# A two-block transformer kernel: latent statistics, state-input steps, one gate tile and two state tables put elsewhere in the second block

## The chip, the cores and the metric

The kernel runs on one core of a Trainium2 chip. The metric is the device time of one execution in microseconds (us). The engines of the core run beside one another and meet only at semaphores: PE (TensorE) multiplies matrices, DVE (VectorE) and ACT (ScalarE) work element by element, POOL (GpSimd) does small and odd work, and SP (SyncE) issues every DMA, in the order of the program. PEld is the loading of weights into PE. The profile also shows the clock that PE was granted: 1.00 is 2.4 GHz, 0.50 is 1.2 GHz.

## The reference

Two blocks follow each other on one sequence of 256 tokens of width 1024. The first (two layers of swiglu, pooling and blockwise attention) is not touched by the change. The second is, cut to what matters here:

```
h = rmsnorm(x) * (1 + scale) + shift
u_s, z_s, q_lat, kv_lat, k_rope, z_m, gl_s, gl_m = split(h @ w_in)
y_s = state_space(u_s)                     # 64 groups, 64 states, chunked scan over time
y_s = ((a * sigmoid(b)) * silu(z_s)) @ w_br_ssm,   [a, b] = gelu(y_s) @ w_glu + b_glu
q = rmsnorm(q_lat) @ w_q_up ;  k, v = rmsnorm(kv_lat) @ w_kv_up      # latent attention
y_m = (attention(q, k, v) * silu(z_m)) @ w_br_mla                    # 16 heads
x = x + gate * rmsnorm((sigmoid(gl_s) * y_s + sigmoid(gl_m) * y_m) @ w_out)
```

All of it is float32. A product of two float32 matrices is made of three matmuls in a reduced format: each operand is split into a high and a low part, and high by high, low by high and high by low are summed in PSUM.

## The kernel before, in words

Activations are held transposed (features on the partitions, 256 tokens along the row). Weights come as tiles of 128x1024 (512 KB): SP loads each into one of five raw buffers (`wraw`, L215), ACT casts the high part (`whi`, L229), DVE subtracts for the low part (`wlo`, L220), and PE uses the pair. `Stream` keeps five raw and five split tiles; a raw buffer is free, and so the next load can be issued, when `wlo` of its tile is done. The order of the tiles is that of the array `w2`, which `prepare` packs. A tile of an ordinary projection (`proj_a`, `mm3`) is 24 matmuls of 256 columns (L356).

`phase2` is the second block. Every engine works through its own list in the order in which the code is written; there is no scheduler. The parts that the change touches, in that order:

1. **The u projection** (L1572 to L1590). Eight weight tiles give `u_s`, in 32 steps p = 0 to 31 of six matmuls each (L368 to L370, `mm3b`), eight steps to each of four column blocks q. Three other things are woven in between these steps. First the statistics of the two latents: `LAT_AT` gives the steps at which the functions of `latent` run. For each latent these are `one` (ACT squares, tiles `stacc` and `stlast`), `two` (`st_half`, PE sums over the partitions, L500), `st_reduce` (PE sums the last square, DVE and POOL make the reciprocal root, L520) and `four` (PE spreads it, L526, DVE and ACT scale the latent and split it into `lhl`). `kfold` (L1539) does the rotary key. Second the state-input steps: `v_steps` is a generator, and `V_RATE[p]` says how many of its steps are taken after step p. For each of four chunks `ch` it has nine steps: four with a group of matmuls of `U` with the table `Gs` (L1554), one with the ACT copy `vt` (L1558), four with a transpose each (L1563); the four ACT copies into `VS` (L1568) and the load of a later table follow with the next step taken. Third `u_evac`: when block q is done, ACT copies it (`us`, L1545) and DVE transposes it into `U` (L1546), which chunk q of the state-input steps reads.
2. **After the last step** the steps that are left run one after the other (L1591 to L1593): all of chunk 3.
3. **The attention** (`mla`). Keys and values are projected from `lhl` (L356 to `mKT`, L368 to `mV`). Then the loop over four groups of heads mixes projections of queries (`q_half`), of the gate z_m (`zm`, eight tiles with psC, L356, then ACT L1873 and DVE L1875) and of the other gate (`gm`) with the steps of sixteen heads (`adv`: scores and softmax, transposition, product with the values L1840). The recurrence of the states runs on POOL beside it (L1600 to L1604).
4. **The branch projection and the z_s projection** (`br_evac`, `zs_step`). `y_mm(ch)` (L1644, L1649) multiplies `U` with the triangular tables `TT[ch // 2]` and the states with the tables `Hs`; it is called in `br_evac` for ch 0 to 2 and in `zs_step` for ch 3 to 7. `TT[0]` and `TT[1]` (`Ta`) are loaded during the attention, `TT[2]` and `TT[3]` (`Tb`) in this part; each takes eight loads (`tload`, L1803) after a memset by POOL (L1618). `tload` of `Tb` is called one at a time in `br_evac` for `TT[2]` and two at a time in `zs_step` for `TT[3]`, so it stands in SP's list among the weight loads and the loads of `Hs` (L1622).

Of the kernel before, what the change touches and what calls it, by code (L numbers as in the profile page):

```python
# [8 lines left out]
F32 = mybir.dt.float32  # L9
# [4 lines left out]
OP = mybir.AluOpType  # L14
# [10 lines left out]
LAG = 1  # L25
LEAD = 7
GRAW = 7
V_RATE = [0] * 9 + ([2, 1] * 3 + [0] * 2) * 2 + [2, 1] * 3 + [0]
HQ = (1, 4)
LAT_AT = (0, 5, 6, 7, 9, 10, 14, 16, 19)  # L30
W_OUT = (1.2, 1.6, 1.5, 1.6)
KV_A = 97
AT_A, AT_Q, AT_O = 150, 0, 2
# [53 lines left out]
def prepare(I):  # L87
# [48 lines left out]
    zmh, quh, gmh = _pack_a(zm), _pack_a(qu), _pack_a(gm)  # L136
    mix = [quh[:1]]
    for i in range(4):
        mix += [zmh[2 * i:2 * i + 1], quh[i + 1:i + 2], zmh[2 * i + 1:2 * i + 2], gmh[i:8 if i == 3 else i + 1]]
    gl = I["w_glu_2"][0].reshape(2, 8, 4, 16, 2048).transpose(0, 2, 1, 3, 4).reshape(1024, 2048)  # L140
    glt = _tiles_a(np.ascontiguousarray(gl))
    glt = glt.reshape(2, 8, 8, 128, 128).transpose(1, 0, 2, 3, 4)
    A["w2"] = np.concatenate(
        [_pack(np.ascontiguousarray(_tiles_a(np.concatenate([ql, kl, krd], 1)).transpose(1, 0, 2, 3))
               .reshape(-1, 128, 128)), _pack_b(us, 256), _pack_a(kn), _pack_b(vv, 512)]
        + mix + [_pack_a(I["w_br_mla_2"][0]), _pack_a(zs), _pack_a(gs),
                 _pack(np.ascontiguousarray(glt).reshape(-1, 128, 128)),
                 _pack_a(I["w_br_ssm_2"][0]), _pack_b(I["w_out_2"][0], 512)], 0)
# [102 lines left out]
class Kernel:  # L251
# [1206 lines left out]
    def phase2(self):  # L1458
# [116 lines left out]
        for q in range(4):  # L1575
            pa = [self.ps("A"), self.ps("B")]
            for k in range(8):
                if k % 4 == 0:
                    hi, lo = self.next()
                p = 8 * q + k  # L1580
                if p in hooks:
                    hooks[p]()
                for x in range(2):
                    self.mm3b(pa[x][:, :256], hp[0][:, k, x], hp[1][:, k, x],
                              flat(hi[:, 2 * (k % 4):2 * (k % 4) + 2]),
                              flat(lo[:, 2 * (k % 4):2 * (k % 4) + 2]), k == 0, k == 7)
                for _ in range(V_RATE[p]):
                    next(vs, 0)
            self.defer(u_evac, q, pa)
        self.flush()  # L1590
        for _ in vs:  # L1591
            pass
        p2v.close()  # L1593
# [1 line left out]
        with self.tc.tile_pool(name="mla", bufs=1) as self.ap:  # L1595
            m = [self.ap.tile([128, 2, 32], F32, name="rm%d" % i, bufs=2) for i in range(2)]
            ar = self.A8[:, 0:1].to_broadcast([128, 2, 32])
            for c in range(31):
                x = XS[:, c]
                PL.tensor_mul(m[0], x, ar)  # L1600
                PL.tensor_mul(m[1][:, 0], x[:, 1], self.A8[:, 1])
                PL.tensor_mul(m[1][:, 1], x[:, 0], self.A8[:, 2])
                PL.tensor_add(m[0], m[0], VS[:, c])
                PL.tensor_add(XS[:, c + 1], m[0], m[1])  # L1604
            PL.tensor_copy(VS[64:, :, 0], XS[:64, :, 1])
            PL.tensor_copy(XS[:64, :, 1], XS[64:, :, 0])
            PL.tensor_copy(XS[64:, :, 0], VS[64:, :, 0])
            self.mla(hh, ll, krs, MM, yy)
        p2a.close()
        pb_ = self.pool("p2b")  # L1610
        zz = pb_.tile([128, KB, T], F32, name="zzs")
# [2 lines left out]
        with self.tc.tile_pool(name="ssy", bufs=2) as sy:  # L1614
            HH = {}
            for c2 in (2, 3):
                TT[c2] = sy.tile([128, 4, 4, 128], F32, name="Tb%d" % c2, bufs=1)
                nc.gpsimd.memset(TT[c2].rearrange("p b j x -> p (b j x)"), 0.0)  # L1618

            def hload(ch):  # L1620
                HH[ch] = sy.tile([128, 2, 512], F32, name="Hs", bufs=3)
                nc.sync.dma_start(HH[ch].rearrange("p b x -> p (b x)"),  # L1622
                                  self.Hd[ch].rearrange("a n g x -> (a n) (g x)"))
            for ch in range(3):
                hload(ch)

            def zs_evac(n, p):
                t = self.tmp.tile([128, T], F32, name="sg", bufs=2)
                S.activation(t, p, AF.Tanh, scale=0.5)
                self.los()  # L1630
                V.scalar_tensor_tensor(zz[:, n], t, 1.0, p, op0=OP.add, op1=OP.mult)
            YF = sy.tile([128, KB, T], F32, name="YF", bufs=1)
            Y = {}

            def y_mm(ch):
                ih, c4 = divmod(ch, 4)
                if c4 == 0:
                    Y[ih] = sy.tile([128, 8, 8, 16], F32, name="YS", bufs=1)
                py = self.ps("A")
                p4 = py[:, :256].rearrange("p (b x) -> p b x", b=2)  # L1640
                for bx in range(2):
                    b = 2 * ch + bx
                    for j in range(4):
                        nc.tensor.matmul(p4[32 * j:32 * j + 32, bx], U[:, 4 * b + j], TT[ch // 2][:, ch % 2 * 2 + bx, j],  # L1644
                                         start=True, stop=False)
                    for j in range(4):
                        q, g2 = divmod(j, 2)
                        x = (g2 * 2 + q) * 128
                        nc.tensor.matmul(p4[32 * j:32 * j + 32, bx], XS[:, :, g2, 2 * b + q],  # L1649
                                         HH[ch][:, bx, x:x + 128], start=False, stop=True)  # L1650
                S.copy(Y[ih][:, :, 2 * c4:2 * c4 + 2].rearrange("p t b x -> p b t x"),
                       p4.rearrange("p b (t x) -> p b t x", t=8))
                if ch + 3 < 8:
                    hload(ch + 3)

            def y_tr(ih):
                for t4 in range(2):
                    pt = self.ps("B")
                    for t in range(4):
                        nc.tensor.transpose(pt[:, t * 128:(t + 1) * 128],  # L1660
                                            Y[ih][:, 4 * t4 + t].rearrange("p b x -> p (b x)"), self.ident)
                    dst = YF[:, 4 * ih:4 * ih + 4].rearrange("p j (c t) -> p t j c", t=8)
                    S.copy(dst[:, 4 * t4:4 * t4 + 4], pt.rearrange("p (t j c) -> p t j c", t=4, j=4))

            GA = {}

            def gelu(i):
                if i:
                    b = sy.tile([128, T], F32, name="gb")
                    S.activation(b, GA[i - 1], AF.Tanh, scale=0.7978845608028654)  # L1670
                if i < KB:
                    a = GA[i] = sy.tile([128, T], F32, name="ga")
                    S.activation(a, YF[:, i], AF.Square)
                self.los()
                if i:
                    g = GA.pop(i - 1)
                    V.scalar_tensor_tensor(g, b, 1.0, YF[:, i - 1], op0=OP.add, op1=OP.mult)
                if i < KB:
                    V.tensor_scalar(a, a, 0.044715, 1.0, op0=OP.mult, op1=OP.add)
                    V.tensor_mul(a, a, YF[:, i])  # L1680
                if i:
                    self.hilo(gg[:, i - 1], g, 0.5)

            def br_evac(n, p):
                V.scalar_tensor_tensor(MM[:, n], MM[:, n], 1.0, p, op0=OP.add, op1=OP.mult)
                self.tload(2, n)
                if n in (3, 5, 7):
                    y_mm(n // 2 - 1)
            self.proj_a(yy, br_evac, tags="CD", late=True)
            self.dump("d_MM", MM)  # L1690

            def zs_step(n, p):
                if n < 4:
                    self.tload(3, 2 * n)
                    self.tload(3, 2 * n + 1)
                if n < 5:
                    y_mm(n + 3)
                if n in (2, 6):
                    y_tr(n // 4)
                zs_evac(n, p)  # L1700
                if n >= 4:
                    gelu(n - 4)
            self.proj_a(hh, zs_step, tags="CD", late=True)

            def gs_evac(n, p):
                S.activation(tg[:, n], p, AF.Tanh, scale=0.5)
                if n < 5:
                    gelu(n + 4)
            self.proj_a(hh, gs_evac, tags="CD", late=True)
# [92 lines left out]
        src = self.Rd[0:16, 4 * c2:4 * c2 + 4, :, :128 - 16 * s]  # L1802
        self.nc.sync.dma_start(tt[16 * s:16 * s + 16, :, 16 * s:], src.rearrange("p b j x -> p (b j) x"))  # L1803

    def mla(self, hh, ll, krs, MM, yy):
        nc, V, S = self.nc, self.nc.vector, self.nc.scalar
        ap = self.ap
        KT = ap.tile([128, 16, T], F32, name="mKT")
# [11 lines left out]
                S.copy(VM[:, th, nch * 512:(nch + 1) * 512], pp[th])  # L1820
        self.proj_b(ll[:, 2:], 2, v_evac, kb=2)
        scale = 96.0 ** -0.5
        Q, Z, P, PT, PO = {}, {}, {}, {}, {}

        def s1(hd):
            sm = self.softmax_a(self.ps("A"), Q[hd], KT[:, hd], 1, lambda th: scale, None)
# [41 lines left out]
            return p[:, :T]  # L1868

        def zm(n):  # L1870
            p = tile8()
            t = self.tmp.tile([128, T], F32, name="sg", bufs=2)
            S.activation(t, p, AF.Tanh, scale=0.5)  # L1873
            Z[n] = ap.tile([128, T], F32, name="zm", bufs=3)
            V.scalar_tensor_tensor(Z[n], t, 1.0, p, op0=OP.add, op1=OP.mult)  # L1875

        def gm(n):
            p = tile8()
# [19 lines left out]
        q_half(0, 0)  # L1898
        q_half(0, 1)
        for grp in range(4):  # L1900
            zm(2 * grp)
            adv()
            if grp < 3:
                q_half(grp + 1, 0)
# [44 lines left out]
```

## Time and profile before

| | |
|---|---|
| median of three runs | 1303.39 us (1303.3 to 1306.41) |
| profiled execution, its own time | 1308.08 us |
| its span, first to last instruction | 1306.3 us |
| PE / PEld busy | 1258.7 us (96%) / 1167.4 us (89%) |
| DVE / ACT / POOL busy | 1015.6 (78%) / 669.4 (51%) / 165.3 us (13%) |
| mean clock granted to PE | 0.987 |
| DMA | 331.14 MB, mean 253 GB/s |

PE's busy time counts overlapping matmuls and is not PE at its peak. What a stage can give is read from PE's waits and from the clock in that stage. A row of the timeline gives start, duration, engine, line and what is worked on, and behind it, in brackets, the time that the engine stood still just before and what ended it. The second block's part that is touched lies between 950 and 1200 us of the span.

### The profile page before, as it was taken

What the parts mean: (1) busy time and instruction counts of PE and PEld (TensorE: products, weight loads), DVE (VectorE), ACT (ScalarE), POOL (GpSimd) and SP (SyncE); (2) the same over time, 40 slices, a digit from 0 to 9 for tenths busy, and PEclk for the clock granted to TensorE, in tenths of its full rate; (3) what the DMA queues carried; (4) which work ended last, traced back from release to release, by engine and by line L of the source; (5) the groups of instructions that cost most, each with busy time, mean ns of one, the idle gap of its engine ahead of it and who ended that gap; (6) DMA issues with size and microseconds to landing.
All of it is one profiled execution on the core that took longest, in us unless ns stands there. A gap on an engine that the chain in (4) does not pass through costs nothing.

```text
span 1306.3 us, 25415 instructions
## 1 busy us (share of the span) xinstructions
PE 1258.7 (96%) x9870; PEld 1167.4 (89%) x9870; DVE 1015.6 (78%) x1768; ACT 669.4 (51%) x1170; POOL 165.3 (13%) x285
## 2 busy tenths in 40 slices
PE   7999999999999999999998999999999899989998
PEld 5999988899988779999886899998888888989997
DVE  6789896789999789999977777878853576537774
ACT  4455444555444665544447555444465855437443
POOL 1000011100002000121111201000210791100000
PEclk9999999899999999999999999999998999989999
DMA  9899996788899568998974478778655544764852
GB/s 365 297 344 386 335 369 237 251 310 259 274 326 332 203 256 299 312 324 301 360 279 145 129 237 268 265 258 282 223 195 172 156 130 124 226 202 143 292 191 81
DMA packets 119850, 331.14 MB, mean 253 GB/s; under 512 B 28273, under 2 KB 39409, under 8 KB 119666
## 3 DMA queue, kind: packets, MB, share of 16 engines
q1 hardware_dynamic: 119730, 329.52, 73.4%
q8 instruction: 77, 1.26, 0.4%
q14 instruction: 43, 0.35, 0.1%
HBM read 317.94 MB, written 10.49 MB: 251 GB/s over the span
## 4 chain that ended last, share of the span: by engine, by line
PE 71%; DVE 4%; ACT 4%; issue 2%; DMA 2%; POOL 1%; SPq 0%; DVEq 0%; ACTq 0%; POOLq 0%
PE psD L356 13%; PE psB L356 12%; PE psA L356 11%; PE psC L356 7%; PE psA L363 5%; PE psB L363 4%; PE psA L364 3%; PE psB L364 2%; DVE wlo L220 1%; PE psA L368 1%; PE psA L369 1%; PE psA L370 1%; PE psB L368 1%; PE psB L370 1%; PE psB L369 1%
## 5 line engine op out<-in xcount | busy, mean ns | idle before, releaser
L220 DVE TENSOR_TENSOR wlo<-wraw,whi 128x1024 fp32r<-128x1024 f32 x391 | 481.3, 1236 | 44.6 <-ACT whi L229 43.4
L229 ACT CAST whi<-wraw 128x1024 fp32r<-128x1024 f32 x391 | 403.1, 1049 | 94.5 <-ACT whi L229 32.7
L356 PE MATMUL psA<-hhl,whi 128*128 128x256 f32 x960 | 247.4, 283 | 4.7 <-ACT hhl L534 4.6
L356 PE MATMUL psB<-hhl,whi 128*128 128x256 f32 x976 | 248.4, 281 | 0.0
L356 PE MATMUL psD<-hhl,whi 128*128 128x256 f32 x1120 | 213.7, 283 | 0.4 <-ACT hhl L534 0.4
L356 PEld LDWEIGHTS psA<-hhl,whi 128*128 128x128 f32 x960 | 180.2, 189 | 7.9 <-ACT hhl L534 6.2
L356 PEld LDWEIGHTS psB<-hhl,whi 128*128 128x128 f32 x976 | 183.8, 190 | 0.0
L389 DVE SCALAR_TENSOR_TENSOR junk<-graw,cb 128x1024 bf16<-128x1024 f32 x146 | 179.3, 1228 | 5.5 <-DMA cb<-in_c 5.5
L356 PEld LDWEIGHTS psD<-hhl,whi 128*128 128x128 f32 x1120 | 178.6, 190 | 2.7 <-issue 1.8
L356 PE MATMUL psD<-hhl,wlo 128*128 128x256 f32 x560 | 157.2, 281 | 0.0
L356 PE MATMUL psB<-hhl,wlo 128*128 128x256 f32 x488 | 136.9, 281 | 0.0
L356 PE MATMUL psA<-hhl,wlo 128*128 128x256 f32 x480 | 134.9, 281 | 1.3 <-DVE wlo L220 1.3
L363 PE MATMUL psA<-shl,whi 128*128 128x512 f32 x352 | 123.8, 392 | 0.0
L356 PEld LDWEIGHTS psD<-hhl,wlo 128*128 128x128 f32 x560 | 106.3, 190 | 0.0
L364 PE MATMUL psA<-shl,wlo 128*128 128x256 f32 x352 | 99.2, 282 | 0.0
L356 PE MATMUL psC<-hhl,whi 128*128 128x256 f32 x480 | 93.4, 286 | 0.4 <-DVE hhl L1456 0.4
L356 PEld LDWEIGHTS psA<-hhl,wlo 128*128 128x128 f32 x480 | 91.2, 190 | 1.7 <-DVE wlo L220 1.7
L356 PEld LDWEIGHTS psB<-hhl,wlo 128*128 128x128 f32 x488 | 92.4, 189 | 0.0
L363 PE MATMUL psB<-shl,whi 128*128 128x512 f32 x264 | 92.2, 390 | 0.0
L484 POOL TENSOR_TENSOR stacc<-stacc,stsq 128x256 f32<-128x256 f32 x33 | 35.1, 1063 | 381.9 <-ACT stsq L479 340.4
L356 PEld LDWEIGHTS psC<-hhl,whi 128*128 128x128 f32 x480 | 77.0, 191 | 3.2 <-issue 2.2
L363 PEld LDWEIGHTS psA<-shl,whi 128*128 128x128 f32 x352 | 66.1, 188 | 14.3 <-issue 0.8
(453 smaller groups left out, 2362.1 us busy)
## 6 DMA issues: line engine op xcount, KB each, us to landing
wraw<-in_win SPq DMA_DIRECT2D x176, 512.0 KB
graw<-in_ada SPq DMA_DIRECT2D x173, 512.0 KB
wraw<-in_w SPq DMA_DIRECT2D x93, 512.0 KB
wraw<-in_wout SPq DMA_DIRECT2D x88, 512.0 KB
wraw<-in_wkv SPq DMA_DIRECT2D x16, 512.0 KB
hg<-in_ada SPq DMA_DIRECT2D x11, 512.0 KB
Hd<-ct SPq DMA_DIRECT2D x64, 64.0 KB
Gd<-gsb SPq DMA_DIRECT2D x16, 256.0 KB
```

Source lines behind the costliest of these rows:

```text
L220: self.nc.vector.tensor_sub(lo, raw, hi.bitcast(F32))
L229: self.nc.scalar.copy(hi, raw)
L356: self.nc.tensor.matmul(*a, skip_group_check=shared, **kw)
L363: mm(out, hi[:, b], a.rearrange("p x t -> p (x t)"), start=first, stop=False)
L364: mm(out[:, :T], lo[:, b], a[:, 0], start=False, stop=last)
L368: mm(out, ah, whi, start=first, stop=False)
L369: mm(out, ah, wlo, start=False, stop=False)
L370: mm(out, al, whi, start=False, stop=last)
L389: self.nc.vector.scalar_tensor_tensor(junk, self.gemv_tile(j), 1.0, self.cb, op0=OP.mult, op1=OP.mult, accum_out=self.modc[:, j:j + 1])
L484: (eng or nc.gpsimd).tensor_add(acc, acc, sq)
```

## The change

The steps of the latent statistics that come after the squares are put later (`LAT_AT`). The state-input steps begin two steps later and come two at a time where they came as 2, 1, 2, 1 (`V_RATE`). The first tile of the gate z_m is computed right after the u projection, into psC, with the rest of the state-input steps inside it, and no longer at the beginning of the attention loop; its evacuation is a function of its own, `zm_evac`, its three buffers lie in the pool `p2a`, and its weight tile stands in `w2` right behind those of u. The last block of u is evacuated directly, not by `defer`. `br_evac` asks for two parts of a `Tb` table in each of its eight calls, `TT[2]` in the first four and `TT[3]` in the last four; `zs_step` asks for none.

```diff
-V_RATE = [0] * 9 + ([2, 1] * 3 + [0] * 2) * 2 + [2, 1] * 3 + [0]
+V_RATE = [0] * 11 + [2, 2, 1, 0, 0, 2, 2, 0] * 2 + [2, 2, 1, 0, 2]
-LAT_AT = (0, 5, 6, 7, 9, 10, 14, 16, 19)
+LAT_AT = (0, 9, 10, 11, 13, 14, 19, 21, 24)
...
-        mix += [zmh[2 * i:2 * i + 1], quh[i + 1:i + 2], zmh[2 * i + 1:2 * i + 2], gmh[i:8 if i == 3 else i + 1]]
+        mix += [zmh[2 * i:2 * i + 1] if i else zmh[:0], quh[i + 1:i + 2], zmh[2 * i + 1:2 * i + 2],
+                gmh[i:8 if i == 3 else i + 1]]
...
-               .reshape(-1, 128, 128)), _pack_b(us, 256), _pack_a(kn), _pack_b(vv, 512)]
+               .reshape(-1, 128, 128)), _pack_b(us, 256), zmh[:1], _pack_a(kn), _pack_b(vv, 512)]
...
-            self.defer(u_evac, q, pa)
-        self.flush()
+            if q < 3:
+                self.defer(u_evac, q, pa)
+        z0 = self.ps("C")
+        hi, lo = self.next()
+        u_evac(3, pa)
+        for k in range(KB):
+            for _ in range({0: 2, 5: 5}.get(k, 0)):
+                next(vs, 0)
+            self.mm3(z0[:, :T], hi, lo, k, hh[:, k], k == 0, k == 7)
+        Z = {}
+        self.zm_evac(Z, pa_, 0, z0[:, :T])
         for _ in vs:
             pass
...
             def br_evac(n, p):
                 V.scalar_tensor_tensor(MM[:, n], MM[:, n], 1.0, p, op0=OP.add, op1=OP.mult)
-                self.tload(2, n)
+                for x in range(2):
+                    self.tload(2 + n // 4, n % 4 * 2 + x)
...
             def zs_step(n, p):
-                if n < 4:
-                    self.tload(3, 2 * n)
-                    self.tload(3, 2 * n + 1)
                 if n < 5:
                     y_mm(n + 3)
...
+    def zm_evac(self, Z, pool, n, p):
+        t = self.tmp.tile([128, T], F32, name="sg", bufs=2)
+        self.nc.scalar.activation(t, p, AF.Tanh, scale=0.5)
+        Z[n] = pool.tile([128, T], F32, name="zm", bufs=3)
+        self.nc.vector.scalar_tensor_tensor(Z[n], t, 1.0, p, op0=OP.add, op1=OP.mult)
...
         for grp in range(4):
-            zm(2 * grp)
+            if grp:
+                zm(2 * grp)
             adv()
```

How the instructions stand on PE behind the last step of the u projection, before. The first row is that step's last matmul, `Gs,U` is chunk 3's group of state-input matmuls (the profile counts each of them as two), `k_ident,vt` its transposes, `lhl,whi` the beginning of the key projection:

```order
L370 MATMUL psB<-whi,hp_11835 128x256
L1554 MATMUL psD<-Gs,U 32x128 x16
L1563 MATMUL psD<-k_ident,vt 128x128 x4
L356 MATMUL psC<-lhl,whi 128x256
L356 MATMUL psC<-lhl,wlo 128x256
```

The same place on PE now; `psC<-hhl` is the gate tile, and lines are one to fifteen higher:

```order
L371 MATMUL psB<-whi,hp_11835 128x256
L1564 MATMUL psD<-k_ident,vt 128x128 x4
L357 MATMUL psC<-hhl,whi 128x256
L357 MATMUL psC<-hhl,wlo 128x256
...
L357 MATMUL psC<-hhl,whi 128x256
L1555 MATMUL psD<-Gs,U 32x128 x16
L357 MATMUL psC<-hhl,whi 128x256
...
L1564 MATMUL psD<-k_ident,vt 128x128 x4
L357 MATMUL psC<-lhl,whi 128x256
```

Five eighths of the gate tile stand between the last step of u and chunk 3's group, and three eighths between this group and its transposes. The first four transposes are chunk 2's; two of them stood among the steps of u before.

How SP's list stands from the end of the branch projection on, before. `Tb_13849` is `TT[3]`, its first load is 16x2048 and its last 16x16x16:

```order
L1622 DMA Hs<-Hd 128x1024
L215 DMA wraw<-in_w 128x1024
L1803 DMA Tb_13849<-Rd 16x2048
L1803 DMA Tb_13849<-Rd 16x16x112
L1622 DMA Hs<-Hd 128x1024
L215 DMA wraw<-in_w 128x1024
L1803 DMA Tb_13849<-Rd 16x16x96
L1803 DMA Tb_13849<-Rd 16x16x80
L1622 DMA Hs<-Hd 128x1024
L215 DMA wraw<-in_w 128x1024
L1803 DMA Tb_13849<-Rd 16x16x64
```

The same loads on SP now; the first `Hs` row here is two `Hs` loads earlier in the list than the first row above:

```order
L1632 DMA Hs<-Hd 128x1024
L216 DMA wraw<-in_w 128x1024
L1811 DMA Tb_13849<-Rd 16x2048
L1811 DMA Tb_13849<-Rd 16x16x112
L216 DMA wraw<-in_w 128x1024
L1811 DMA Tb_13849<-Rd 16x16x96
L1811 DMA Tb_13849<-Rd 16x16x80
L1632 DMA Hs<-Hd 128x1024
L216 DMA wraw<-in_w 128x1024
L1811 DMA Tb_13849<-Rd 16x16x64
L1811 DMA Tb_13849<-Rd 16x16x48
```

All eight loads of `TT[3]` moved ahead of the last three loads of `Hs`, by four weight loads.

## Rows read from the trace of the kernel before

**Rows 1.** Waits of PE, 950 to 1200 us: total us, times, longest us.

```profile
PE psD L1563 <- ACT vt L1558: 2.6, 2, 1.5
PE psD L1840 <- ACT smpt L909: 2.2, 2, 1.3
```

**Rows 2.** Busy time by stretch: us, PE, PEld, DVE, ACT, POOL, clock, DMA share, GB/s.

```profile
974.00:978.00 4.00, 1.90 (x10) 1.50 (x9) 1.22 (x1) 3.90 (x9) 0.00 (x0) 0.84 0.25 102
978.00:982.00 4.00, 4.00 (x16) 3.13 (x16) 0.00 (x0) 1.41 (x2) 0.00 (x0) 0.50 0.43 131
982.00:986.00 4.00, 4.00 (x19) 4.00 (x20) 2.17 (x4) 0.74 (x2) 2.29 (x2) 0.50 0.24 51
986.00:990.00 4.00, 4.00 (x50) 3.02 (x48) 2.62 (x5) 1.44 (x4) 0.00 (x0) 0.88 0.52 174
```

**Rows 3.** Timeline of PE, u projection: start, duration, line, work, wait before it.

```profile
976.74 1.01 PE L500 MATMUL psC<-ones,stacc 128*128 128x1 f32 x4 [2.09 <-ACT stacc L473]
...
995.11 0.28 PE L368 MATMUL psA<-whi,hp 128*128 128x256 f32 x1
...
995.92 0.64 PE L1554 MATMUL psD<-Gs,U 128*32 128x128 f32 x16
996.49 0.39 PE L368 MATMUL psA<-whi,hp 128*128 128x256 f32 x1
...
997.39 0.43 PE L1554 MATMUL psD<-Gs,U 128*32 128x128 f32 x8
997.75 0.43 PE L526 MATMUL psC<-k_ident,strs 128*128 128x128 f32 x2
```

**Rows 4.** Timeline of ACT in the u projection and behind it.

```profile
976.56 0.43 ACT L471 ACTIVATE stlast<-lat 128x256 f32<-128x256 f32 x1
...
1012.82 2.46 ACT L1568 COPY VS<-psD 64x256 f32<-64x256 f32 x4
```

**Rows 5.** Timeline of PE behind the last step of u.

```profile
1012.24 0.28 PE L370 MATMUL psB<-whi,hp 128*128 128x256 f32 x1
1013.77 1.08 PE L1554 MATMUL psD<-Gs,U 128*32 128x128 f32 x32 [1.26 <-issue]
1015.94 0.66 PE L1563 MATMUL psD<-k_ident,vt 128*128 128x128 f32 x4 [1.09 <-ACT vt L1558]
1016.36 0.37 PE L356 MATMUL psC<-lhl,whi 128*128 128x256 f32 x1
```

**Rows 6.** Chain that ended last, start of the attention loop: start, duration, what.

```profile
1032.68 2.81 PE psC L356 x24
...
1036.35 0.28 DVE smx L884
```

**Rows 7.** Timeline of DVE, same place.

```profile
1032.67 1.35 DVE L1894 TENSOR_TENSOR mQ<-psD,CS 64x512 f32<-64x512 f32 x2 [1.11 <-ACT mQ L1893]
```

**Rows 8.** Timeline of PE, z_s projection, groups of y_mm.

```profile
1151.51 0.43 PE L1644 MATMUL psA<-Ta,U 128*32 128x128 f32 x8
...
1155.55 0.43 PE L1644 MATMUL psA<-Tb,U 128*32 128x128 f32 x8
...
1169.04 0.65 PE L1644 MATMUL psA<-Tb,U 128*32 128x128 f32 x8 [4.55 <-DMA Tb<-Rd]
...
1175.60 0.43 PE L1644 MATMUL psA<-Tb,U 128*32 128x128 f32 x8
```

**Rows 9.** Timeline of SP, z_s projection.

```profile
1157.55 0.91 SPq L1803 DMA_DIRECT2D Tb<-Rd  x2
...
1165.05 0.92 SPq L1803 DMA_DIRECT2D Tb<-Rd  x2
```

**Rows 10.** Busy time by stretch, branch and z_s projections.

```profile
1126.00:1138.00 12.00, 12.00 (x127) 11.71 (x126) 5.82 (x8) 4.01 (x5) 0.79 (x1) 1.00 1.00 269
1150.00:1162.00 12.00, 12.00 (x171) 11.13 (x169) 2.87 (x3) 1.82 (x4) 0.00 (x0) 1.00 1.02 294
```

**Rows 11.** Timeline of POOL, memsets of the Tb tables.

```profile
1123.22 3.57 POOL L1618 MEMSET Tb<- 128x2048 f32 x2 [39.82 <-DVE sf L1844]
```

More of the change, by code (lines that the diff above doesn't have):

```diff
@@ L1607, in phase2 @@
             PL.tensor_copy(XS[64:, :, 0], VS[64:, :, 0])
-            self.mla(hh, ll, krs, MM, yy)
+            self.mla(hh, ll, krs, MM, yy, Z, pa_)
         p2a.close()
@@ L1803, in tload, with mla @@
         self.nc.sync.dma_start(tt[16 * s:16 * s + 16, :, 16 * s:], src.rearrange("p b j x -> p (b j) x"))
-    def mla(self, hh, ll, krs, MM, yy):
+    def zm_evac(self, Z, pool, n, p):
[3 more added lines that the diff above has]
+        self.nc.vector.scalar_tensor_tensor(Z[n], t, 1.0, p, op0=OP.add, op1=OP.mult)
+    def mla(self, hh, ll, krs, MM, yy, Z, zpool):
         nc, V, S = self.nc, self.nc.vector, self.nc.scalar
@@ L1822, in mla @@
         scale = 96.0 ** -0.5
-        Q, Z, P, PT, PO = {}, {}, {}, {}, {}
+        Q, P, PT, PO = {}, {}, {}, {}
         def s1(hd):
@@ L1870, in zm @@
         def zm(n):
[L1871 to L1875, printed above, removed]
+            self.zm_evac(Z, zpool, n, tile8())
         def gm(n):
```

## The prediction

> **What bounds the kernel now.** I read PE's waits in the stretch of the change first, then the clock stretch by stretch, then the timeline of PE at each wait, and only then the engines that PE waits for. In most of the stretch PE runs without a gap at 2.4 GHz; what the change can give back is where it does not, and there are four such places.
>
> First, the u projection. Behind step 4 PE stands still for 2.09 us until ACT has the first square of a latent [rows 3], and right behind this gap the granted clock falls to 0.50 and stays low for some ten us [rows 2]. Second, two waits for the ACT copy `vt`, 2.6 us in all, the longer (1.5) inside the u projection and the other 1.09 behind it [rows 1, 5]. Third, chunk 3 of the state input runs alone behind the last step of u: from 1012.4 (1012.24 and one matmul pitch) to 1016.36 PE works 1.1 + 0.4 us and stands still for 1.26 + 1.09 [rows 5]. Fourth, one group of `y_mm` waits 4.55 us for the last two loads of `TT[3]` [rows 8], which SP issued only at 1165.05, 7.5 us after the pair before [rows 9]; in between stands a weight load in SP's list, so the tables are late by the order, not by the transfer.
>
> **Part 1, the statistics.** The sum that stopped PE moves from step 5 to step 9. A step is six matmuls; with the seam to a group it takes 0.81 us (995.11 to 995.92 [rows 3]), without it about 0.71, so from 974.65, where PE stopped (976.74 less 2.09), four steps end at 977.5. ACT was done with the first square when it began the second at 976.56 [rows 4]. The wait goes, with 0.9 us to spare: -2.1. What is next late is POOL's root, which PE needs two steps later, as before, now with two groups of state input in between; I price it at nothing, and at most at one wait like the one removed (+2).
>
> With the wait goes what followed it. Time lost to the clock is the stretch times one minus the clock: 4 x (0.16 + 0.50 + 0.50 + 0.12) = 5.1 us [rows 2]. This stretch held almost only matmuls back to back, so lost clock was lost time: -5.1. The whole part: -7.2. Bounds: -2.1 if the clock falls anyway, -7.5 if some pieces beside it shrink too.
>
> The trace shows the clock falling behind a gap of 2.09 us, while the gap of 1.5 us and the pair of 1.26 and 1.09 left it at 1.00. The Trainium skill (TensorE: Matmul & The Clock Gate, Why this matters for your kernels) blames only gaps longer than this one for throughput drops within a kernel. By that rule the slow stretch would have another cause and the part would give 2.1, not 7.2. The rows decide for 7.2 in the sum; the other result is the first rival.
>
> **Part 2, steps in bunches.** A group of 16 matmuls between two steps: from step to step 995.11 to 996.49, 1.38 us. A group of 8: 996.49 to 997.75, 1.26 us [rows 3]. Without the 0.71 of the step (0.81 less the seam of 0.1) that is 0.67 and 0.55. A chunk had 16 + 8 + 8 = 1.77 and has 16 + 16 = 1.34, three chunks: -1.3. The transposes come as 2, 2 and not as 1, 2, 1; they cost 0.1 to 0.2 each way and I leave them at nothing. Bounds 0 and -1.8.
>
> **Part 3, the waits for `vt` inside u.** Before: 1.5 us, in chunk 1. Now two steps without state input lie between the copy and the transposes, 1.4 us for a copy of 0.6. But ACT takes its list in order: in chunk 0 the copies of the scaled latent stand ahead of `vt`, in chunk 2 the four `VS` copies (2.46 us together [rows 4]) and a cast do. Laying the rows' durations one behind the other I get a wait of 0.6 in the first and 0.4 in the last. 1.5 goes, 1.0 comes: -0.5. Bounds -1.5 and +1.5 (two waits as long as the longest of before).
>
> **Part 4, the gate tile.** A tile is 2.81 us [rows 6]. Behind the last step of u PE now has a pair of transposes (0.2), the tile, chunk 3's group (1.1 and 0.2 for seams), four transposes (0.4), and the wait for `vt`. ACT's chain there is two `us` copies, the four `VS` copies of 2.46 and `vt` of 0.6, begun some 0.9 us later behind a cast: it ends about when the tile does, so 0.2 of wait is left. Sum 4.9 against 4.0 before: +0.9 until the key projection begins. In return the attention loop begins without 2.81 of PE. It does not give all: the first softmax needs the queries, and DVE ends their second product at 1034.02 (1032.67 + 1.35 [rows 7]), while the first maximum began at 1036.35, behind the gate tile's evacuation [rows 6]. ACT and DVE carry the chain from there to the product with the values, where PE waits 1.3 [rows 1]; so the gain is 1036.35 - 1034.05 = 2.3. Net -1.4. Bounds: +0.9 (the loop gains nothing) and -2.35 (all that PE stood still in [rows 5]).
>
> **Part 5, the tables.** All loads of `TT[3]` are issued by the end of the branch projection, and POOL's memsets end at 1126.8 [rows 11], long before the first of them. The wait of 4.55 goes. So does what the clock lost: from group to group 1169.04 to 1175.60 = 6.56 us, where the same work took 1151.51 to 1155.55 = 4.04 [rows 8]: 2.5. Together -7.1. Nothing is late in its place by my reading: the last two `Hs` loads stay where they were relative to PE, with fewer loads ahead of them. The cost is on the DMA engines, busy at 1.00 while the branch projection runs [rows 10]: eight loads of 16 to 128 KB, 576 KB in all, are 2.0 us at the 294 GB/s of [rows 10], in a stage whose weights are asked for up to ten tiles ahead (five raw, five split). Taken as nothing. Bounds of the part 0 and -7.1.
>
> **Sum.** -7.2 - 1.3 - 0.5 - 1.4 - 7.1 = -17.5 us. The profiled execution took 1308.08 (its span 1306.3 and 1.8 around it), 4.7 above the median; the change would make it 1290.6. The terms are differences within one execution, so I take them off the median: 1303.39 - 17.5 = **1285.9 us**.
>
> **Rivals.** *The clock is not given back in u*: the short waits of part 3 and the thin sums bring it down again at another place, or its cause was not the gap. For it: PE's gaps there were many; against: gaps of 1.5 and of 1.26 and 1.09 did nothing. 1285.9 + 5.1 = 1291.0. *The attention loop takes the tile back*: with no gate tile as cover, PE waits for the queries and then for the values; the 2.3 are lost, 1288.2, and 1291 if the wait for the values (1.3) grows to the two us behind which the clock fell. For it: ACT and DVE carry that chain; against: they lose the tile's evacuation and a split as well. *The table wait changes its name*: `y_mm` waits for `Hs` or for ACT's evacuation for half as long: 1285.9 + 3.5 = 1289.4. Against: these loads are issued early and the queue is emptier. *Slower, the weights starve*: the eight loads moved into the branch projection hold the DMA queue there, and the weight loads behind them come late. A load costs at most 3.1 us, from the end of SP's last pair at 1165.97 to PE's restart at 1169.04 [rows 8, 9]. Were each to push the full queue back by that, 24.8 us: 1285.9 + 24.8 = 1310.7. It decides from 17.5 / 8 = 2.2 us a load on. Against: 0.25 us each by bytes, and the lead. The rows of these loads have 512 bytes or less (64 to 448 for all but the first). The Trainium skill (DMA: Bandwidth & Descriptors, Specifications) says that transfers below 512 B miss line rate; no row here gives their share of the engines, and only this raises the rival from next to nothing.
>
> **How the numbers follow.** My forecast, 1285.9 give or take 3: 0.55. Everything at its better bound, some 3.5 further down, 1282: 0.08. Clock in u: 0.13. Attention loop: 0.12. Table wait renamed: 0.08. Starved weights: 0.03; the last 0.01 for no effect. Half-clock stretches outside the change can move a few us from run to run, so the range goes from 1280 to 1293. Faster, that is by over 0.3% (3.9 us, about what a measurement of this kernel tells from no change): 0.95; within it 0.02; slower 0.03.
>
> **What would show it.** In the trace after: no gap before L501 in the u projection and a clock of 1.00 from its first step to its last; groups of 16 there, each under 0.7 us; waits for `vt` under a microsecond; the key projection beginning some 8 to 9 us earlier than 1016.4, and the wait for the values still about 1.3; no wait for `Tb` and 4.0 us from group to group of `y_mm`. I am wrong if the clock is below 1 anywhere in u, if a wait for `Hs`, `wraw` or `wlo` shows up from the branch projection on, or if the attention loop gives back less than a microsecond.

## The result, and the profile of the changed kernel

The changed kernel takes 1289.28 us (median of four executions, 1285.92 to 1290.54), the kernel before on the same chip 1303.35 (four, 1301.05 to 1306.41): a ratio of 0.9889, 95% interval 0.9866 to 0.9911, or 14.1 us less (11.6 to 17.5 by that interval). Forecast were 1285.9, that is 17.5 less, and a range of 1280 to 1293. The profiled execution of the changed kernel took 1289.56 us, its span is 1287.7, its mean granted clock 0.994. PE is busy for 1250.8 us (97%), PEld 1161.1, DVE 1014.7, ACT 669.0, POOL 168.5.

The waits of PE of half a us or more that are left between 950 and 1200 us are these (what waits and for whom: us in total, times, longest us):

```profile
PE psD L1854 <- ACT smpt L910: 1.3, 1, 1.3
PE psC L357 <- ACT mKT L1829: 0.9, 1, 0.9
PE psA L880 <- DVE mQ L1904: 0.7, 1, 0.7
PE psD L1564 <- ACT vt L1559: 0.6, 1, 0.6
PE psD L357 <- ACT VS L1569: 0.5, 1, 0.5
```

The 2.09 for `stacc` [rows 3] and the 4.55 for `Tb` [rows 8] are gone, and of the two waits for `vt` [rows 1] one of 0.6 is left. The stretch that ran at half clock [rows 2] reads now (us, PE, PEld, DVE, ACT, POOL, clock, DMA share, GB/s):

```profile
974.00:978.00 4.00, 4.00 (x33) 3.66 (x31) 2.32 (x2) 4.00 (x9) 0.00 (x0) 1.00 0.05 6
978.00:982.00 4.00, 4.00 (x51) 3.41 (x54) 2.15 (x4) 1.78 (x4) 2.28 (x2) 1.00 0.77 261
982.00:986.00 4.00, 3.51 (x38) 3.11 (x30) 2.77 (x5) 1.30 (x4) 0.00 (x1) 1.00 0.48 145
```

PE in the u projection, behind it and in the z_s projection (start, duration, line, work, and in brackets the wait before it), against [rows 3, 5, 8]:

```profile
954.45 0.38 PE L357 MATMUL psD<-hhl,whi 128*128 128x256 f32 x1 [0.35 <-ACT hhl L535]
...
976.25 0.50 PE L501 MATMUL psC<-ones,stacc 128*128 128x1 f32 x4
...
986.16 0.44 PE L1564 MATMUL psD<-k_ident,vt 128*128 128x128 f32 x2 [0.64 <-ACT vt L1559]
...
989.32 0.64 PE L1555 MATMUL psD<-Gs,U 128*32 128x128 f32 x16
...
1002.16 0.66 PE L1564 MATMUL psD<-k_ident,vt 128*128 128x128 f32 x4
1002.57 0.36 PE L357 MATMUL psC<-hhl,whi 128*128 128x256 f32 x1
...
1004.56 1.08 PE L1555 MATMUL psD<-Gs,U 128*32 128x128 f32 x32
...
1006.75 0.60 PE L1564 MATMUL psD<-k_ident,vt 128*128 128x128 f32 x4
1007.10 0.36 PE L357 MATMUL psC<-lhl,whi 128*128 128x256 f32 x1
...
1024.22 0.49 PE L880 MATMUL psA<-mKT,mQ 128*128 128x128 f32 x2 [0.75 <-DVE mQ L1904]
...
1038.26 0.65 PE L1854 MATMUL psD<-smpt,mV 128*64 128x256 f32 x2 [1.29 <-ACT smpt L910]
...
1140.10 0.42 PE L1654 MATMUL psA<-Ta,U 128*32 128x128 f32 x8
...
1144.14 0.43 PE L1654 MATMUL psA<-Tb,U 128*32 128x128 f32 x8
...
1153.02 0.43 PE L1654 MATMUL psA<-Tb,U 128*32 128x128 f32 x8
...
1157.03 0.43 PE L1654 MATMUL psA<-Tb,U 128*32 128x128 f32 x8
```

The sums of the squares run without a wait (976.25). The gate tile fills what stood empty between the last step of u and the key projection, which now begins at 1007.10. On DVE the first maximum of the attention loop begins 11.0 us earlier than in [rows 6]:

```profile
1025.35 0.29 DVE L885 TENSOR_REDUCE smx<-psA 128x1 f32<-128x128 f32 x1 [0.53 <-PE psA L883]
```

SP issues the last two loads of `TT[3]` 28.3 us earlier than in [rows 9]:

```profile
1136.71 1.19 SPq L1811 DMA_DIRECT2D Tb<-Rd  x2
```

Walking from mark to mark gives the balance of the two profiled executions. The first mark, a matmul ahead of the change, stood at 955.53 in the trace of before:

```profile
955.53 0.39 PE L356 MATMUL psD<-hhl,whi 128*128 128x256 f32 x1 [0.36 <-ACT hhl L534]
```

So 1.1 us was there already at 954.45. The key projection is 9.3 earlier (1016.36 [rows 5]), the first maximum 11.0, the first group of `y_mm` shown 11.4, the last 18.6 (1175.60 [rows 8]). Part by part: u and what lies behind it -8.2, the start of the loop -1.7, the rest of the attention -0.4, the tables -7.2, and the 1.1 that is not the change's. The spans differ by 18.6, the touched stretch by 17.5.

### The profile page after: what moved, and what is told of

It is laid out like the page before. It is cut to its first block, busy times and chain, and to the rows that moved or that the text cites. A ratio compares the mean times of both kernels' runs of the same rounds, so it can differ in the third digit from the quotient of the medians.

```text
span 1287.7 us, 25411 instructions
## 1 busy us (share of the span) xinstructions
PE 1250.8 (97%) x9870; PEld 1161.1 (90%) x9870; DVE 1014.7 (79%) x1768; ACT 669.0 (52%) x1170; POOL 168.5 (13%) x285
## 3 DMA queue, kind: packets, MB, share of 16 engines
q8 instruction: 77, 1.26, 0.4%
## 4 chain that ended last, share of the span: by engine, by line
PE 70%; ACT 4%; DVE 4%; issue 2%; DMA 2%; POOL 1%; SPq 0%; DVEq 0%; ACTq 0%; POOLq 0%
PE psD L357 13%; PE psB L357 12%; PE psA L357 11%; PE psC L357 7%; PE psA L364 5%; PE psB L364 4%; PE psA L365 3%; PE psB L365 2%; DVE wlo L221 1%; PE psA L369 1%; PE psA L370 1%; PE psA L371 1%; PE psB L371 1%; PE psB L370 1%; PE psB L369 1%
## 5 line engine op out<-in xcount | busy, mean ns | idle before, releaser
L596 ACT CAST shl<-sf 128x256 fp32r<-128x256 f32 x88 | 35.8, 407 | 85.9 <-DVE sf L594 85.9
```

Of the source, the lines that this page charges most:

```text
L596: nc.scalar.copy(ss[:, i, 0], s)
```

## The experiments

Twelve runs follow, two of them of the kernels before and after as they are, each timed beside the kernel before on the same chip. Ratios are to that, with their 95% interval; 0.001 is 1.3 us, and gains in us are worked out from the ratios. Where two ratios are compared, the difference is uncertain by some 0.003, or 4 us. In eight of the others a single part was put into the kernel before, or taken out of the changed one; the two named last go beyond the change.

**The kernel before, once more.** No edit.

> The kernel before, unchanged, to see how much of its time differs from run to run. Theory (the clock differs from run to run): ratio within 0.997 to 1.003 of itself, single executions 1301 to 1308 us, and an execution is longer by what its granted clock is lower: 1.3 us for each 0.001 of the mean clock. In the trace the two gaps (2.1 us before L500 in the u projection, 4.5 us before L1644) are there again, and the half-clock stretches behind them may be shorter than the 10 and 7 us of the first profile, or absent. Rival (the profile of before was typical, and the 4 us between its own time and the median come from elsewhere): the same half-clock stretches, 10 and 7 us, in this trace too, and a mean clock of 0.987 in every execution.

1303.82 us, ratio 0.9995 [0.9982, 1.0009]. Its profiled execution took 1303.14 us at a clock of 0.993. The gap is the same, and behind it the clock (first a row of PE's timeline, then stretches as above):

```profile
974.67 0.61 PE L500 MATMUL psC<-ones,stacc 128*128 128x1 f32 x4 [2.09 <-ACT stacc L473]
```

```profile
974.00:978.00 4.00, 3.33 (x20) 2.87 (x20) 1.22 (x1) 3.08 (x6) 0.00 (x0) 0.87 0.31 89
978.00:982.00 4.00, 4.00 (x29) 3.87 (x31) 2.68 (x5) 1.13 (x4) 2.29 (x2) 0.70 0.29 93
1010.00:1014.00 4.00, 3.17 (x16) 3.17 (x17) 0.00 (x0) 2.94 (x6) 0.74 (x3) 0.64 0.18 39
1014.00:1018.00 4.00, 3.75 (x29) 3.53 (x29) 1.24 (x1) 3.83 (x10) 3.33 (x9) 0.94 0.85 163
```

Behind the 2.09 the clock took 4 x (0.13 + 0.30) = 1.7 us and not 5.1; and behind the pair of 1.25 and 1.1, which did nothing in the first trace, it took another 1.7. What a gap costs in clock differs from one execution to the next. Over the 61 executions of before that belong to these runs the median is 1304.81 us at a clock of 0.989 (1297.72 to 1309.81); the 9 at 0.987 took 1307.15 on the mean, the 4 at 0.993 took 1301.16. That is 1.0 us for each 0.001 of clock, where 1.3 was expected, and a wider spread than expected.

**The statistics alone.**

```diff
-LAT_AT = (0, 5, 6, 7, 9, 10, 14, 16, 19)
+LAT_AT = (0, 9, 10, 11, 13, 14, 19, 21, 24)
```

> Only the statistics are moved (LAT_AT of the changed kernel, all else as before). Theory (gap brings the clock down): no gap before L500, clock 1.00 through the u projection, 7.2 us less than an execution like the profiled one; against the median of before 3 to 7 us less (ratio 0.9945 to 0.998). Rival (the slow clock has another cause): the gap goes but the clock falls in the u projection all the same, 2.1 us less (0.998 to 0.999).

1306.04 us, ratio 1.0011 [0.9997, 1.0025]: nothing gained. The 2.09 goes, but PE waits elsewhere:

```profile
977.56 0.65 PE L1554 MATMUL psD<-Gs,U 128*32 128x128 f32 x16 [1.58 <-DVE U L1546]
...
988.83 0.65 PE L1554 MATMUL psD<-Gs,U 128*32 128x128 f32 x16 [1.87 <-issue]
```

```profile
988.02 0.71 DVE L1546 STREAM_TRANSPOSE U<-us 128x512 f32<-128x512 f32 x1 [1.67 <-ACT us L1545]
```

```profile
990.00:994.00 4.00, 4.00 (x31) 2.93 (x30) 0.00 (x0) 0.34 (x1) 0.00 (x0) 0.56 0.70 258
994.00:998.00 4.00, 4.00 (x20) 4.00 (x20) 1.30 (x2) 2.48 (x3) 1.40 (x1) 0.50 0.00 0
```

State-input steps that still begin at step 9 find `U` late: the second group starts when DVE's transposition (the row at 988.02) is done. Behind its wait of 1.87 the half clock comes, a dozen us further on than before, and takes 5.1 us again. The transposition itself waited for ACT's copy `us`, so PE, no longer held up by `stacc`, meets the same list of ACT a few steps later.

**The statistics with a later start.** The new `LAT_AT`, and the old pattern of state-input steps two steps later.

```diff
-V_RATE = [0] * 9 + ([2, 1] * 3 + [0] * 2) * 2 + [2, 1] * 3 + [0]
+V_RATE = [0] * 11 + ([2, 1] * 3 + [0] * 2) * 2 + [2, 1, 2, 0, 2]
```

> The kernel before with the new LAT_AT and with its own 2, 1, 2, 1 pattern begun at step 11 instead of 9: neither bunches, gate tile nor tables. Theory (the statistics can move only because the state-input steps begin two steps later; with step 9 the groups waited for the table U, which DVE made late between the scaled latents): no gap of 2.09 before L500, no wait for U over half a us inside the u projection, the granted clock 1.00 there unless a wait for vt of about 1.5 lowers it; 2 to 6 us under before, ratio 0.995 to 0.9985. Rival (moving the statistics is worth nothing by itself, whatever the state-input steps do): U late as in the run with the statistics alone, ratio within 0.9985 to 1.0025.

1299.33 us, ratio 0.9958 [0.9945, 0.9971], 5.5 us less. The theory holds in what it says of PE: no gap before L500, no wait for `U`. That DVE was late between the scaled latents is not what the trace above shows: DVE stood idle there, waiting for ACT. Two waits stand in the trace none the less, and the clock stayed up behind both:

```profile
985.24 0.33 PE L1563 MATMUL psD<-k_ident,vt 128*128 128x128 f32 x1 [1.51 <-ACT vt L1558]
...
1005.92 1.08 PE L1554 MATMUL psD<-Gs,U 128*32 128x128 f32 x32 [2.10 <-DMA Gs<-Gd]
```

```profile
1002.00:1006.00 4.00, 1.90 (x20) 1.64 (x22) 1.82 (x2) 3.82 (x8) 0.00 (x0) 1.00 0.67 235
1006.00:1010.00 4.00, 3.25 (x51) 2.98 (x51) 0.00 (x0) 2.39 (x5) 0.74 (x3) 1.00 0.05 12
```

The wait for `Gs`, chunk 3's table, is new. Its load is issued with the step after chunk 1's transposes, and the group that reads it now comes sooner behind that.

**The changed kernel with the old `LAT_AT`.**

> The changed kernel with the old places of the statistics (LAT_AT of before). Theory: the gap of 2.1 us before L501 is back and behind it a stretch at half clock of 3 to 10 us; 2.1 + 1.7 to 5.1 = 3.8 to 7.2 us more than the changed kernel. Rival (clock has another cause): gap back, clock 1.00, 2.1 us more.

1295.86 us, ratio 0.9933 [0.9911, 0.9954]: 0.0044 above the changed kernel's 0.9889, 5.7 us. The gap of 2.09 is back, with the clock at 0.75, 0.50, 0.50 and 0.97 in the four stretches from 974 us (two of them shown), which is 5.1 us of clock again. The later start of the state-input steps is in this kernel, so by itself it doesn't remove the gap.

```profile
976.29 1.01 PE L501 MATMUL psC<-ones,stacc 128*128 128x1 f32 x4 [2.09 <-ACT stacc L474]
```

```profile
978.00:982.00 4.00, 4.00 (x16) 3.13 (x16) 0.00 (x0) 1.41 (x2) 0.00 (x0) 0.50 0.41 131
982.00:986.00 4.00, 4.00 (x19) 4.00 (x20) 2.62 (x5) 0.83 (x3) 2.29 (x2) 0.50 0.32 93
```

**The bunches alone**, begun at step 9 as before.

```diff
+V_RATE = [0] * 9 + [2, 2, 1, 0, 0, 2, 2, 0] * 2 + [2, 2, 1, 0, 2, 2, 0]
```

> Only the state-input steps come in bunches (2, 2, 1, 0, 0, 2, 2, 0 where they came as 2, 1, 2, 1, 2, 1, 0, 0, from the same step on; all else as before). Theory: three groups of 8 less, 1.3 us less, and the wait for vt in chunk 1 (1.5 us) goes or shrinks to 0.6: 1.3 to 2.8 us less (ratio 0.998 to 0.999), which is near what can be measured; read it in the trace from the first group to the last step of u. Rival (bunches cost what they save, through ACT's order): 0 (1.000).

1303.33 us, ratio 0.9986 [0.9973, 0.9999], 1.8 less, what parts 2 and 3 came to together, and by the interval anything from 0.1 to 3.5. The one wait for `vt` that is left inside u is 0.64. In its profiled execution, the shortest of its twelve at 1299.95, the 2.09 gap (ending at 974.61) had no half clock behind it at all; behind u the clock took 1.7 us:

```profile
974.00:978.00 4.00, 3.39 (x24) 2.93 (x25) 1.29 (x2) 3.08 (x6) 0.00 (x0) 1.00 0.30 90
978.00:982.00 4.00, 3.58 (x40) 3.05 (x40) 3.55 (x6) 1.26 (x4) 2.28 (x2) 1.00 0.43 159
```

**The changed kernel with 2, 1, 2, 1 from step 11.**

> The changed kernel with the state-input steps as 2, 1, 2, 1 again, from the same step on as in it. Theory: groups of 16, 8 and 8 for 16 and 16, 0.44 us more for a chunk, 1.3 us more for three, and waits for vt between 0 and 1.5 us each: 1.3 to 3 us more than the changed kernel. Rival: 0.

1290.63 us, ratio 0.9892 [0.9869, 0.9914]. The wait for `vt` is back at 1.51, but the time is within 0.0003 of the changed kernel's. The bunches gave 0.4 here and 1.8 above, which can't be told from nothing here and hardly there; what counts in `V_RATE` is the later start.

**The changed kernel without the gate tile behind u.** The old tail, the old place in `w2`:

```diff
-            if q < 3:
-                self.defer(u_evac, q, pa)
-        z0 = self.ps("C")
...
+            self.defer(u_evac, q, pa)
+        self.flush()
...
-            if grp:
-                zm(2 * grp)
+            zm(2 * grp)
```

> The changed kernel with the gate tile back at the beginning of the attention loop, and the last steps of the state input alone behind the u projection, as before. Theory: 1.4 us more than the changed kernel by my sum (1.0 by its trace: 0.9 lost behind u, 1.8 won at the loop), and PE's gaps behind the last step of u back: 1.3 and 1.1 us. The remaining steps there are two transposes more than before. Rival (the attention loop takes the tile back): 0.9 us less.

1290.59 us, ratio 0.9898 [0.9875, 0.992], 1.2 more, against 1.4 forecast; by the intervals it could be nothing. Its trace shows what the tile covers:

```profile
1003.81 1.08 PE L1555 MATMUL psD<-Gs,U 128*32 128x128 f32 x32 [1.51 <-DMA Gs<-Gd]
1005.64 0.66 PE L1564 MATMUL psD<-k_ident,vt 128*128 128x128 f32 x4 [0.75 <-ACT vt L1559]
```

Not `U` and `vt` alone, as I had it, but the table's load as well; in exchange the wait of 0.75 for `mQ` at the start of the loop is absent here.

**The tables alone** (the `br_evac` and `zs_step` part of the diff in the kernel before).

> Only the table loads are moved (two in each call of br_evac, none in zs_step; all else as before). Theory: no wait before L1644, 4.0 us from group to group of y_mm, 7.1 us less than an execution like the profiled one, 4.6 to 7.1 less in the median (ratio 0.9945 to 0.9965). Rival (the wait changes its name: Hs, ACT or the weights): a wait of 2 us or more somewhere from the branch projection on, 3.5 us less or nothing (0.997 to 1.0). Rival (weights starve): slower.

1297.13 us, ratio 0.9936 [0.9919, 0.9954], 8.3 less. No wait for `Tb`, `Hs`, `wraw` or `wlo` from the branch projection on. The groups of `y_mm` are 4.0 us apart, as in the changed kernel's rows above, and 4.8 where a transposition of 1.1 us lies between, in both kernels.

**The changed kernel with the old order of the tables.**

> The changed kernel with the old table loads (one in each call of br_evac, two in zs_step). Theory: the wait of 4.5 us before L1654 is back, and behind it a stretch at half clock; 4.6 to 7.1 us more than the changed kernel. Rival (the wait came from the slow clock before it, and is gone with it): 0 to 2 us more.

1295.08 us, ratio 0.993 [0.9908, 0.9952], 5.3 more. The wait is back in full, with 10 x (0.07 + 0.10) = 1.7 us of clock behind it. The next group comes 5.6 us later (at 1163.88) and not 4.0, so 1.5 of this counts, where the sum had 2.5:

```profile
1158.32 0.45 PE L1654 MATMUL psA<-Tb,U 128*32 128x128 f32 x8 [4.53 <-DMA Tb<-Rd]
```

```profile
1150.00:1160.00 10.00, 5.47 (x65) 4.91 (x65) 3.29 (x4) 4.97 (x8) 0.00 (x0) 0.93 0.62 178
1160.00:1170.00 10.00, 10.00 (x102) 9.71 (x100) 5.45 (x11) 5.25 (x12) 0.00 (x0) 0.90 0.27 68
```

**The changed kernel, once more.**

> The changed kernel as it is, for comparison with the two above: 1288 to 1291 us, ratio 0.986 to 0.991. Theory (the part of the gain that the sum missed is what the clock costs, and that differs between executions of before): before's executions spread over 5 us or more, these over less, at a mean clock of 0.993 to 0.997. Rival (the sum missed a wait): no difference in spread, and a waiting place of over a us that the first profile did not show.

1289.82 us (1286.15 to 1290.46), ratio 0.9883 [0.9866, 0.9901]. Theory and rival both find something. The clock of its executions lies at 0.993 to 0.995 (0.993 to 0.997 with the first four), above nearly all of before, and in both profiles it is 1.00 from 966 to 1200 us. The spread doesn't tell them apart: 4.3 us here, 4.5 for before beside it. And there is a wait of over a us that the first profile did not have:

```profile
1005.55 1.08 PE L1555 MATMUL psD<-Gs,U 128*32 128x128 f32 x32 [1.45 <-DMA Gs<-Gd]
```

SP's list there, of this execution and then of the first one of the changed kernel:

```profile
989.65 7.14 SPq L216 DMA_DIRECT2D wraw<-in_w  x3
996.84 1.32 SPq L1495 DMA_DIRECT2D Gs<-Gd  x1
```

```profile
997.31 1.72 SPq L1495 DMA_DIRECT2D Gs<-Gd  x1
```

From SP's beginning the issue to the use is 7.25 us in the first execution, without a wait, and 8.7 with the 1.45 here. Before, SP began at 999.09 (the repeated kernel before) and the group ran at 1008.66, 9.6 later. The table now comes just in time or up to 1.5 us late.

**DVE takes part of ACT's copies.** From the last steps of u to 1024 us ACT works with one pause of 0.36 us; DVE gets two copies into `VS` and every second one into `mKT`.

```diff
-            S.copy(KT[0:64, 2 * n + 1], p[64:128])
+            V.tensor_copy(KT[0:64, 2 * n + 1], p[64:128])
...
-                        S.copy(VS[64 * g2:64 * g2 + 64, :, a, 8 * ch:8 * ch + 8].rearrange("p c i -> p i c"),
+                        (V.tensor_copy if ch == 3 and a else S.copy)(
+                            VS[64 * g2:64 * g2 + 64, :, a, 8 * ch:8 * ch + 8].rearrange("p c i -> p i c"),
```

> The changed kernel, with every second copy into mKT (L1829) and two of chunk 3's four copies into VS on DVE instead of ACT; ACT is busy without a pause from 998.6 to 1024 us there, DVE idle for half of it and more. Theory (from u to the attention loop PE now follows ACT's list): the waits of 0.48 (VS) and 0.88 (mKT) and the 0.75 for mQ go, 1 to 2.1 us under the changed kernel. Rival (DVE's copies stand before wlo in its list and make the split tiles late): a wait for wlo of about the same size takes their place, within 0.5 us of the changed kernel.

1288.09 us (1285.93 to 1289.09), ratio 0.9872 [0.9854, 0.9889]: 1.7 under the run above in the medians, within the intervals. In the trace the wait for `mQ` is gone, the others change their name and hardly shrink:

```profile
1010.09 0.36 PE L357 MATMUL psD<-lhl,whi 128*128 128x256 f32 x1 [0.65 <-DVE VS L1569]
...
1011.59 0.39 PE L357 MATMUL psC<-lhl,whi 128*128 128x256 f32 x1 [0.55 <-DVE mKT L1830]
...
1037.44 0.65 PE L1855 MATMUL psD<-smpt,mV 128*64 128x256 f32 x2 [1.59 <-ACT smpt L910]
```

0.65 + 0.55 + 1.59 = 2.8 stands against 0.48 + 0.87 + 0.77 + 1.32 = 3.4 in the run above. The wait for `Gs` is 0.41 in this trace and 1.45 in that, and this 1.0, which the edit doesn't explain, is more than the 0.6 of the others. The run is below both kernels, and faster than the changed one by no more than can be told.

**The same, with the first latent scaled one step later.**

```diff
+LAT_AT = (0, 9, 10, 11, 14, 15, 19, 21, 24)
```

> As the one before, and the scaling of the first latent one step later (LAT_AT 14, 15 for 13, 14), so that the copy vt of chunk 0 stands ahead of the casts of the scaled latent in ACT's list. Theory (the new wait for vt in chunk 0 is ACT's order): the 0.64 there goes, 0.5 to 0.7 us less than without it. Rival (vt is late for its own length, or the casts then delay the copies into VS and chunk 1): no difference, 0 to +0.7.

1288.09 us, ratio 0.9873 [0.986, 0.9887]: no difference. The wait for `vt` in chunk 0 (0.64 in the changed kernel, 0.65 in the run above) goes, so it was ACT's order, and one of 0.63 comes before chunk 1's group at 989.01. The rival's time holds.

## Why the prediction was right, and what it mis-sized

**The mechanisms** came as forecast, and in the trace nearly their sizes: the touched stretch of the two profiled executions differs by the 17.5 of the sum. u and what lies behind it gave 8.2 (forecast 7.2 + 1.3 + 0.5 - 0.9 = 8.1), the tables 7.2 (7.1). That the sum is met to a tenth is partly luck: the start of the loop gave 0.6 too little, and the rest of the attention, which stood in no part, 0.4. Of the four rivals of other times the second came in part (part 4), the others did not: the clock is 1.00 through u, no table wait took another name, no weight load starved.

**The step that failed** is in the sum: "The terms are differences within one execution, so I take them off the median." The two terms of clock, 5.1 and 2.5, are what that one execution paid. Behind the same 2.09 the clock took 5.1 us in three traces (the first, the tables alone, the changed kernel with the old `LAT_AT`), 1.7 in one and nothing in one; in the last two the pair of waits behind u took another 1.7. Behind the wait for `Tb` the next group of `y_mm` came 5.4 to 6.7 us later in the six traces that have this wait, and not 4.0: 1.4 to 2.7 us of clock. So by my estimate, the means of these five and six traces, a typical execution of before had some 5 us of clock to give back at the two places (3.4 + 1.9), and not 7.6: the profiled one was itself 4.7 above the median shown and 3.3 above that of the 61. Two profiles of before differ by 4.9 (1308.08 and 1303.14): 2.1 is there ahead of the change (976.74 [rows 3] and 974.67), 3.7 come up in the touched stretch, mostly from the clock, and 0.8 goes again behind it. Off its own time the sum gave 1290.6, and 1289.28 and 1289.82 were measured. The other piece that is missing is the wait for `Gs`, 0 to 1.5 us (part 4). The two, some 2.3 and up to 1.5, could account for the 3.4 us by which the forecast was too low. But the measured interval reaches the forecast, so how much of the 3.4 is noise stays open.

**Part 1**, forecast 7.2, measured 5.5 put in (with the later start) and 5.7 taken out. Both fall short of 7.2 by no more than their uncertainty. I priced it as if the statistics were free to move by themselves. By themselves they gained nothing, for then `U` is late: the part needs the start two steps later, which is in `V_RATE` and which no part of the sum gave a price.

**Parts 2 and 3**, forecast 1.8: 1.8 put in, 0.4 taken out. The wait of 0.6 for `vt` in chunk 0 came as worked out; the one of 0.4 in the last chunk is the 0.2 to 0.3 before 1002.16.

**Part 4**, forecast 1.4: 1.2 taken out, not told from nothing. The loop gave 1.7 and not 2.3: PE now waits 0.75 for `mQ`, the second rival on a small scale. Behind the last step stand all four transposes of chunk 2 (the row at 1002.16), where the sum has a pair; before, all four, and not two, stood among the steps of u. What I left out is the load of `Gs`: I followed the matmuls and copies of the steps that move, and not the load that they issue. State-input steps that begin later shorten the time from its issue to its use by 2.3 us (9.6 to 7.25; it is 7.2 with the 2, 1, 2, 1 pattern too), and the wait of 0 to 1.5 us that follows is in no part of the sum.

**Part 5**, forecast 7.1: 8.3 put in, 5.3 taken out, 7.2 in the trace. The wait of 4.4 to 4.6 stands in every trace with the old order and in none with the new, and the clock behind it is worth 1.4 to 2.7.

**The clock.** My rule from one trace was: 2.09 brings it down, 1.5 and the pair of 1.26 and 1.09 do not. It doesn't hold. 2.09 in one execution and 2.10 for `Gs` in another left the clock at 1.00; the 1.87 of the statistics alone took 5.1 us, and the pair took 1.7 us in three of the five traces that have it (0.64 on the mean of four us in the repeated kernel before). The Trainium skill (TensorE: Matmul & The Clock Gate, Why this matters for your kernels) blames only longer gaps than any of these; four of the five traces with the gap of 2.09 speak against it, the fifth agrees. What decides between executions stays open: in the two profiles of before the gaps, the work and the order were the same.

## What to carry to other kernels

Take a sum of differences off the time of the execution that they were read from, and ask of each term whether another execution would show it; most waits here repeat to one or two tenths of a us (the one for `Gs`, a load that comes just in time, does not), what the clock adds behind them does not, and a second profile of the same kernel tells the two apart. Where steps are moved, list the loads that they issue, and compare the time from issue to use before and after. And where two parts of a change were put in together, test whether one alone does anything: here the first was worth nothing without two steps of the second.

## What was not expected of the hardware

The same gap of 2.09 us cost 5.1 and 1.7 us of clock in two executions of the same kernel, and nothing in one whose state-input steps came in bunches behind it; the 61 executions of before lie between 1297.72 and 1309.81 us, by and large the longer, the lower their mean clock. SP's issue of chunk 3's `Gs` load took 0.43 us before, and with the later start 1.3 to 1.7 in five profiles and 0.43 in four; three weight loads stand right ahead of it in the five and in three of the four. What sets it, no run here shows.
